# The attention pieces' plain fp32 products side by side, and one split product for the row of negative maxima

## The chip, the cores and the metric

The kernel runs on one core of a Trainium2 chip. The metric is the device time of one execution in microseconds; smaller is better. Of the kernel before there are three runs: 497.45, 497.55 and 498.71 us, median 497.55 us. Beside them stands one profiled execution, from which all rows below come.

## The reference, cut to what matters

One layer of a decoder trunk on 256 positions of width 1024. What touches the change is the mixer:

```python
proj = x @ w_in + b_in            # q_m k_m v_m o_m i_m f_m q_b k_b v_b g_a g_b
# mLSTM branch: 4 heads x 256, stabilised by a running maximum m_q
s   = (q @ k.T) * exp(d_intra - m_q)
num = s @ v ;  den = s.sum(-1)
h   = num / maximum(abs(den), exp(-m_q))
y_a = sigmoid(o_m) * head_norm(h)
# attention branch: 8 heads x 128, one block, causal, with a relative bias
p   = softmax(q @ k.T * scale + bias)
y_b = p @ v
merged = sigmoid(g_a) * (y_a @ w_branch_a) + sigmoid(g_b) * (y_b @ w_branch_b)
x = layer_norm(alpha * x + merged @ w_out)
x = layer_norm(alpha * x + conv_gated_mlp(x))
```

All of it is in fp32. With one layer and no state carried in, the maximum of a position is a running maximum over positions, one row of 256 numbers for each mLSTM head.

## The kernel before, in words

**Numbers.** A matmul in plain fp32 takes several passes on TensorE. For the large products the kernel therefore cuts each fp32 operand into a high part (rounded to the type float32r) and a low part (what is left), and adds three products of one pass: high x high, high x low and low x high. The helper `split_into` makes the parts: ScalarE (ACT in the profile) casts the high part, line 91, and VectorE (DVE) subtracts, line 92. The helper `mm3` issues the three products, lines 125 to 127. A few small products and all transposes stay plain fp32.

**Weights.** They come as 81 chunks of 1 MB in the order of `chunk_order`: four of the output gate `o`, then for each of four groups the eight chunks `qm, qb, km, kb, vm, vb, ga, gb`, then the branch products `wa, wb`, the output product `wo`, and the feed-forward chunks `up` and `dn`. SyncE (SP) issues their loads into three raw buffers, five chunks ahead (line 86). Each step of the loop in `run` first issues the element work (`elem_work`: what is left of the step before, and the splits of the chunk two steps ahead), then the load, then the chunk's 48 matmuls, and at the end the small TensorE pieces that `side_pe` holds for this step. The order of instructions on an engine is the order in which the program writes them.

**Start.** Before the loop, `run` loads x and the first chunks in pieces, splits chunks 0 and 1 (line 235) and issues the small loads. The identity matrix `ident` (line 225) is loaded by POOL's queue, behind two broadcasts of bias rows (lines 220 and 221), which wait for their own load. After them POOL clears some tiles, among them `nM` (line 274). The splits of chunk 2 come with the first `elem_work` of the loop.

**A group.** A group is two attention heads and one mLSTM head; its eight steps are b to b+7. The maxima are made once, in the first group, by `gates_schedule`: `e1d` (lines 566 to 570) writes the negated row of each head into partitions 0 to 3 of `nM`. In each group the small pieces are:

- at the end of step b+4: `pe_m` (line 603) lays the group's row on all 128 partitions by one plain product with a column of `ident`; `pe_s` makes the scores of the mLSTM head, of which the block of the later half is plain (line 612); `pe_l(0)` the logits of the first attention head, whose own block is plain (line 711)
- at the end of b+5: `pe_l(1)` for the second head, and `pe_n`, scores x v
- at the end of b+6: `pe_t`, six transposes of the probabilities (line 744)
- at the end of b+7: `pe_y`, four transposes of the mLSTM output (line 695), then `pe_o`, probabilities x v, where each head has one plain product between its split ones (lines 760 to 763)
- in the element work of b+8: `el_y`, then `el_o`, which evacuate these two for the branch products. In the last group b+8 is the first `wa` step, which reads the result of `el_y`.

The side products use five PSUM banks in turn (`ps_side`), the large ones three (`ps_main`).

**Memory.** Pools lie on top of each other from the left: `const` first, then `stream` (raw and split chunks), then the others. `yah, yal, ybh, ybl` and the split parts of the first two `up` chunks lie in pools on the right side. Tiles that TensorE reads carry pads, which the helper `after` and the function `shift` set.

Of the kernel before, what the change touches and what calls it, by code (L numbers as in the profile page):

```python
# [69 lines left out]
class Kernel:  # L70
# [103 lines left out]
    def run(self):  # L174
# [95 lines left out]
        self.cbuf = mp.tile([P, 2, S + 3], F32, name="cbuf")  # L270
        g.memset(self.cbuf[:, :, 0:3], 0.0)

        self.nM = mp.tile([P, S], F32, name="nM")
        g.memset(self.nM, 0.0)
        self.toe = mp.tile([P, 2, S], F32, name="toe")
        self.cv = {n: mp.tile([P, 2, S], F32, name="cv" + n) for n in ("qm", "km")}
        self.ones4 = xp.tile([4, 2 * S], F32, name="ones4")
# [249 lines left out]
    def gates_schedule(self, bif):  # L527
        nc, mp = self.nc, self.xp
        st = {}
        v = nc.vector  # L530

        def e0():
            gt = mp.tile([P, 2, 8], F32, name="gt")
            for t in range(2):
                v.tensor_add(gt[:, t, :], self.psg[t][:, 256:264], bif)
            st["gt"] = gt

        def p0():
            ps = self.ps_side([4, 2, S], "ps_gt")
            for w in range(2):  # L540
                for t in range(2):
                    nc.tensor.transpose(ps[:, w, t * P:(t + 1) * P], st["gt"][:, t, 4 * w:4 * w + 4], self.ident)
            st["ps"] = ps

        def e1():
            ps = st["ps"]
            big = mp.tile([P, KT, S], F32, tag="xraw", name="gates")
            fs, t1, F, G, M, nFM, nM = (big[0:4, k, :] for k in range(7))
            v.tensor_copy(fs, ps[:, 1, :])
            v.scalar_tensor_tensor(t1, fs, -1.0, fs, op0=ALU.mult, op1=ALU.min)  # L550
            nc.scalar.activation(t1, t1, AF.Exp)
            nc.scalar.activation(t1, t1, AF.Ln, bias=1.0)
            st["g"] = fs, t1, F, G, M, nFM, nM

        def e1b():
            fs, t1, F, G, M, nFM, nM = st["g"]
            one = self.ones4[:, 0:S]
            v.scalar_tensor_tensor(fs, fs, 0.0, t1, op0=ALU.min, op1=ALU.subtract)
            v.tensor_tensor_scan(F, one, fs, 0.0, op0=ALU.mult, op1=ALU.add)

        def e1c():
            fs, t1, F, G, M, nFM, nM = st["g"]
            v.tensor_sub(G, st["ps"][:, 0, :], F)
            v.tensor_tensor_scan(M, self.ones4[:, S:2 * S], G, 0.0, op0=ALU.max, op1=ALU.max)

        def e1d():
            fs, t1, F, G, M, nFM, nM = st["g"]
            v.tensor_scalar(self.nM[0:4, :], M, -1.0, None, op0=ALU.mult)
            v.scalar_tensor_tensor(nFM, F, -1.0, M, op0=ALU.mult, op1=ALU.subtract)
            st.update(G=G, nFM=nFM)  # L570

        def p1():
            ps = self.ps_side([P, 2, 2, 4], "ps_gc")
            for w, n in enumerate(("G", "nFM")):
                for t in range(2):
                    nc.tensor.transpose(ps[:, w, t, :], st[n][:, t * P:(t + 1) * P], self.ident[0:4, 0:4])
            st["gc"] = ps

        def e2():
            self.gcol = self.const.tile([P, 2, 4], F32, name="gcol")  # L580
            self.floor = self.const.tile([P, 2, 4], F32, name="floor")
            v.tensor_copy(self.gcol, st["gc"][:, 0])
            self.floor_exp = lambda: nc.scalar.activation(self.floor, st["gc"][:, 1], AF.Exp)

        b = self.start_g[0]
        self.side_elem.setdefault(b, []).append(e0)
        self.side_pe.setdefault(b, []).append(p0)
        self.mixed[b + 1] = lambda w: w + [None, None, e1]
        self.mixed[b + 2] = lambda w: w + [e1b, None, e1c, None, e1d]
        self.side_pe.setdefault(b + 3, []).append(p1)  # L590
        self.mixed[b + 4] = lambda w: w + [e2]


    def group_schedule(self, g):
# [5 lines left out]
        def pe_m():  # L600

            psw = self.ps_side([P, S], f"psw{g}")
            nc.tensor.matmul(psw, self.ident[:, g:g + 1].to_broadcast([P, P]), self.nM, start=True, stop=True)
            st["psw"] = psw

        def pe_s():
            qh, ql = self.hl["qm"]
            kh, kl = self.hl["km"]
            pss = self.ps_side([P, 2, S], f"pss{g}")

            for k in range(2):
                nc.tensor.matmul(pss[:, 0, P:], self.cv["km"][:, k, P:], self.cv["qm"][:, k, P:],
                                 start=k == 0, stop=k == 1)
            for k in range(2):
                self.mm3(pss[:, 1, :], kh[:, k, 0:P], kl[:, k, 0:P], qh[:, k, :], ql[:, k, :], k == 0, k == 1)
            st["pss"] = pss
# [81 lines left out]
        def el_y():  # L698
            for j in range(2):
# [3 lines left out]
                v.scalar_tensor_tensor(self.yal[:, c, :], st["psy"][:, j, :], gain, self.yah[:, c, :].bitcast(F32),  # L703
                                       op0=ALU.mult, op1=ALU.subtract)

        def pe_l(i):
            qh, ql, qf = self.qb
            kh, kl = self.hl["kb"]
            ps = self.ps_side([P, 2, S], f"psl{g}_{i}")

            nc.tensor.matmul(ps[:, 0, 0:P], qf[:, i, :], self.kbf[:, i, :], start=True, stop=True)
            self.mm3(ps[:, 1, :], qh[:, i, :], ql[:, i, :], kh[:, i, :], kl[:, i, :], True, True)
            st["l", i] = ps

        def el_l(i):
            h = 2 * g + i
# [34 lines left out]
            a.copy(tf, ps[:, 2, :])  # L751

        def pe_o():
            ps = self.ps_side([P, 2, S], f"pso{g}")
            vh, vl, vf = self.vb
            for i in range(2):
                th, tl, tf = self.pt[i]
                c = slice(i * P, (i + 1) * P)
                mm = nc.tensor.matmul
                mm(ps[:, i, :], vh[:, c], th, start=True, stop=False)  # L760
                mm(ps[:, i, P:], vf[:, c], tf, start=False, stop=False)
                mm(ps[:, i, :], vh[:, c], tl, start=False, stop=False)
                mm(ps[:, i, :], vl[:, c], th, start=False, stop=True)
            st["o"] = ps

        def el_o():
            ps = st["o"]
            for i in range(2):
                h = 2 * g + i
                bias = self.vec[:, V_BVB + h:V_BVB + h + 1]  # L770
                a.activation(self.ybh[:, h, :], ps[:, i, :], AF.Identity, bias=bias)
                v.scalar_tensor_tensor(self.ybl[:, h, :], ps[:, i, :], bias, self.ybh[:, h, :].bitcast(F32),
                                       op0=ALU.add, op1=ALU.subtract)

        def at(where, k, f):
# [6 lines left out]
        at(self.side_pe, 4, pe_m)  # L782
        at(self.side_pe, 4, pe_s)
        at(self.side_pe, 4, lambda: pe_l(0))
        at(self.side_pe, 5, lambda: pe_l(1))
        at(self.side_pe, 5, pe_n)
        self.mixed[b + 5] = lambda w: [w[0], el_w, lambda: el_l(0), w[1], lambda: el_e(0), el_s, lambda: el_l2(0),
                                       el_s2] + w[2:]
# [2 lines left out]
        at(self.side_pe, 6, lambda: pe_t(0))  # L791
        at(self.side_pe, 6, lambda: pe_t(1))
        self.mixed[b + 6] = lambda w: [lambda: el_l(1), lambda: el_e(1), el_n1] + w + [lambda: el_l2(1), el_n1b]
        at(self.side_pe, 7, pe_y)
        at(self.side_pe, 7, pe_o)
        self.mixed[b + 7] = lambda w: [lambda: el_t(0), el_n2, lambda: el_t(1)] + w
        at(self.side_elem, 8, el_y)
        at(self.side_elem, 8, el_o)


    def open_post(self, pp):
# [375 lines left out]
```

## Time and profile before

| what | value |
|---|---|
| runs | 497.45, 497.55, 498.71 us; median 497.55 |
| span of the profiled execution | 495.6 us, 9471 instructions |
| the profiled execution's own time | its span of 495.6 us, and by the median 1.9 us around it |
| PE (TensorE matmul) busy | 484.4 us, 98% of the span |
| DVE busy, ACT busy, POOL busy | 369.2, 288.5, 29.1 us |
| split product, one pass, 128x256 in `wa` | 64 records, mean 276 ns each, overlapping |
| plain product of the row, 128x256 | two records each, 8 in four groups, mean 378 ns |
| plain product or transpose, 128x128 | mean 272 to 274 ns for a record |

A record's length on PE holds its way through the array, which the next one overlaps. What one matmul costs is therefore read from start to start, or from the chain of waits, where each piece stands with what it adds. The page's 40 slices show PE at nine tenths or more from the second slice on to the last but one.

### The profile page before, as it was taken

To read this page: it belongs to the slowest core of one execution; us is meant where nothing else is said; L and a number is where in the kernel's file an instruction comes from. 1 tells how busy PE (TensorE), PEld (TensorE's weight loads), DVE (VectorE), ACT (ScalarE), POOL (GpSimd) and SP (SyncE) were. 2 spreads that over 40 slices of the span, in tenths; PEclk is the share of its full clock that TensorE was granted. 3 is DMA by queue.
4 is the path that set the end of the run, shared out by engine and by line. 5 is a ranking of instruction groups with operands and counts; after the bars stand their busy time and mean duration, and the time that the engine had idled before them with its cause. 6 is when DMAs were issued, how large, how long until landed. Compare 5 with 4: busy or idle time off the path is not lost.

```text
span 495.6 us, 9471 instructions
## 1 busy us (share of the span) xinstructions
PE 484.4 (98%) x3889; PEld 468.0 (94%) x3889; DVE 369.2 (74%) x662; ACT 288.5 (58%) x479; POOL 29.1 (6%) x46
## 2 busy tenths in 40 slices
PE   8999999999999999999999999999999999999992
PEld 4899999999999999999999999999999999999982
DVE  5676995888588858885677788888667766866886
ACT  6567867496658665866655524766554555554610
POOL 0400011001100110002000001000000000000001
PEclk9999999999999999999999999999999999999998
DMA  8984555556554645443945572646555456444202
GB/s 251 351 305 153 202 197 200 175 173 193 184 184 171 196 172 196 172 171 136 371 176 179 221 280 86 255 145 212 203 206 175 165 181 245 170 171 171 86 1 85
DMA packets 19036, 93.74 MB, mean 189 GB/s; under 512 B 4625, under 2 KB 5913, under 8 KB 9009
## 3 DMA queue, kind: packets, MB, share of 16 engines
q1 hardware_dynamic: 14834, 87.08, 49.2%
q0 software_dynamic: 4160, 6.07, 3.9%
q8 instruction: 30, 0.49, 0.4%
q14 instruction: 12, 0.10, 0.1%
HBM read 92.05 MB, written 2.63 MB: 191 GB/s over the span
## 4 chain that ended last, share of the span: by engine, by line
PE 94%; DMA 2%; DVE 1%; SPq 1%; ACT 0%; issue 0%; POOL 0%; POOLq 0%
PE ps_up L127 8%; PE ps_up L126 8%; PE ps_up L125 8%; PE ffn L127 4%; PE ffn L126 4%; PE ffn L125 4%; PE ps_vm L125 2%; PE ps_vm L127 2%; PE ps_qm L125 2%; PE ps_vm L126 2%; PE ps_ga L127 1%; PE ps_ga L125 1%; PE ps_vb L126 1%; PE ps_vb L127 1%; PE ps_vb L125 1%; PE ps_ga L126 1%
## 5 line engine op out<-in xcount | busy, mean ns | idle before, releaser
L92 DVE TENSOR_TENSOR wl<-raw,wh 128x1024 fp32r<-128x1024 f32 (+1 forms) x162 | 187.5, 1197 | 29.2 <-ACT wh L91 29.0
L91 ACT CAST wh<-raw 128x1024 fp32r<-128x1024 f32 (+1 forms) x162 | 158.8, 1030 | 11.6 <-DMA raw<-in_wst_dram 6.3
L127 PE MATMUL ps_up<-x1h,wl 128*128 128x256 f32 x320 | 89.9, 281 | 0.0
L126 PE MATMUL ps_up<-x1l,wh 128*128 128x256 f32 x320 | 89.9, 281 | 0.0
L125 PE MATMUL ps_up<-x1h,wh 128*128 128x256 f32 x319 | 89.7, 281 | 0.0
L126 PEld LDWEIGHTS ps_up<-x1l,wh 128*128 128x128 f32 x320 | 61.4, 192 | 0.0
L127 PEld LDWEIGHTS ps_up<-x1h,wl 128*128 128x128 f32 x320 | 60.1, 188 | 0.0
L125 PEld LDWEIGHTS ps_up<-x1h,wh 128*128 128x128 f32 x319 | 59.9, 188 | 0.0
L1010 DVE SCALAR_TENSOR_TENSOR cu<-ps_up,vec,cu 128x255 f32<-128x255 f32 (+1 forms) x80 | 33.0, 475 | 27.1 <-ACT cu L1006 26.9
L127 PE MATMUL ffn<-wh,hl 128*128 128x512 f32 (+1 forms) x110 | 38.4, 349 | 0.0
L126 PE MATMUL ffn<-wl,hh 128*128 128x512 f32 (+1 forms) x110 | 38.4, 349 | 0.0
L125 PE MATMUL ffn<-wh,hh 128*128 128x512 f32 (+1 forms) x110 | 38.3, 349 | 0.0
L91 ACT CAST hh<-cu 128x256 fp32r<-128x256 f32 x22 | 8.9, 407 | 42.8 <-DVE cu L1018 42.8
L1006 ACT ACTIVATE cu<-ps_up,vec 128x256 f32<-128x256 f32 x40 | 16.8, 472 | 28.8 <-PE ps_up L127 28.0
L126 PEld LDWEIGHTS ffn<-wl,hh 128*128 128x128 f32 x110 | 20.8, 189 | 3.0
L125 PEld LDWEIGHTS ffn<-wh,hh 128*128 128x128 f32 x110 | 20.7, 188 | 3.0
L127 PEld LDWEIGHTS ffn<-wh,hl 128*128 128x128 f32 x110 | 20.7, 188 | 2.9
L125 PE MATMUL ps_gb<-xth,wh 128*128 128x256 f32 x64 | 18.0, 282 | 0.0
L126 PE MATMUL ps_vm<-wl,xth 128*128 128x256 f32 x64 | 17.9, 280 | 0.0
L127 PE MATMUL ps_vm<-wh,xtl 128*128 128x256 f32 x64 | 17.9, 280 | 0.0
L125 PE MATMUL mix<-wh,mgh 128*128 128x256 f32 x64 | 17.8, 279 | 0.0
L125 PE MATMUL ps_qm<-xth,wh 128*128 128x256 f32 x64 | 17.8, 278 | 0.0
(295 smaller groups left out, 1428.9 us busy)
## 6 DMA issues: line engine op xcount, KB each, us to landing
raw<-in_wst_dram SPq DMA_DIRECT2D x78, 1024.0 KB, 4.9
raw<-in_wst_dram SPq DMA_DIRECT2D x8, 256.0 KB, 4.5
lnrow<-in_rows_dram POOLq DMA_DIRECT2D x4, 512.0 KB, 7.5
band<-table POOLq DMA_DIRECT2D x4, 384.0 KB, 13.0
xraw<-in_xt_dram SPq DMA_DIRECT2D x8, 128.0 KB, 4.3
raw<-in_wst_dram SPq DMA_DIRECT2D x2, 512.0 KB, 7.6
toe<-band POOLq DMA_DIRECT2D x4, 256.0 KB, 4.2
xtok<-in_x_dram POOLq DMA_DIRECT2D x1, 1024.0 KB, 8.3
```

The source lines that it names most:

```text
L91: self.nc.scalar.copy(wh, raw)
L92: self.nc.vector.tensor_sub(wl, raw, wh.bitcast(F32))
L125: mm(ps, ah if first is None else first, bh, start=start, stop=False)
L126: mm(ps, ah, bl, start=False, stop=False)
L127: mm(ps, al, bh, start=False, stop=stop)
L1006: act.activation(cu[:, j, :], ps[:, j, :], AF.Copy, scale=tap(2, j))
L1010: v.scalar_tensor_tensor(cu[:, j, o:], ps[:, j, :S - o], tap(t, j), cu[:, j, o:], op0=ALU.mult, op1=ALU.add)
```

## The change

- `nM` becomes float32r. `e1d` writes the negated row into a plain tile, ACT copies its high part into partitions 0 to 3 of `nM`, and DVE subtracts and writes the low part into partitions 32 to 35. A new tile `pick` of four columns, in the `const` pool, has a one in row g and in row 32 + g of column g; DVE makes it at the start by adding two slices of `ident`. `pe_m` then is one float32r product, which adds high and low part.
- The own blocks of both heads' logits go behind the plain part of the scores (`pe_l_own`, called in `pe_s`), and `pe_l(1)` moves from step b+5 to b+4.
- `pe_o` has one PSUM tile for each head and issues the split products of both heads, then the two plain ones; `pe_y` comes after it. `el_o` comes before `el_y`.

```diff
-        self.nM = mp.tile([P, S], F32, name="nM")
-        g.memset(self.nM, 0.0)
+        self.nM = mp.tile([P, S], F32R, name="nM")
+        g.memset(self.nM.bitcast(F32), 0.0)
+        self.pick = const.tile([P, 4], F32R, name="pick")
+        nc.vector.tensor_add(self.pick, ident[:, 0:4], ident[:, 32:36])
...
         def e1d():
             fs, t1, F, G, M, nFM, nM = st["g"]
-            v.tensor_scalar(self.nM[0:4, :], M, -1.0, None, op0=ALU.mult)
+            v.tensor_scalar(nM, M, -1.0, None, op0=ALU.mult)
+            nc.scalar.copy(self.nM[0:4, :], nM)
+            v.tensor_sub(self.nM[32:36, :], nM, self.nM[0:4, :].bitcast(F32))
             v.scalar_tensor_tensor(nFM, F, -1.0, M, op0=ALU.mult, op1=ALU.subtract)
...
-            nc.tensor.matmul(psw, self.ident[:, g:g + 1].to_broadcast([P, P]), self.nM, start=True, stop=True)
+            nc.tensor.matmul(psw, self.pick[:, g:g + 1].to_broadcast([P, P]), self.nM, start=True, stop=True)
...
+            for i in range(2):
+                pe_l_own(i)
             for k in range(2):
                 self.mm3(pss[:, 1, :], kh[:, k, 0:P], kl[:, k, 0:P], qh[:, k, :], ql[:, k, :], k == 0, k == 1)
...
+        def pe_l_own(i):
+            ps = st["l", i] = self.ps_side([P, 2, S], f"psl{g}_{i}")
+            nc.tensor.matmul(ps[:, 0, 0:P], self.qb[2][:, i, :], self.kbf[:, i, :], start=True, stop=True)
+
         def pe_l(i):
             qh, ql, qf = self.qb
             kh, kl = self.hl["kb"]
-            ps = self.ps_side([P, 2, S], f"psl{g}_{i}")
-
-            nc.tensor.matmul(ps[:, 0, 0:P], qf[:, i, :], self.kbf[:, i, :], start=True, stop=True)
-            self.mm3(ps[:, 1, :], qh[:, i, :], ql[:, i, :], kh[:, i, :], kl[:, i, :], True, True)
-            st["l", i] = ps
+            self.mm3(st["l", i][:, 1, :], qh[:, i, :], ql[:, i, :], kh[:, i, :], kl[:, i, :], True, True)
...
         def pe_o():
-            ps = self.ps_side([P, 2, S], f"pso{g}")
+            ps = [self.ps_side([P, S], f"pso{g}_{i}") for i in range(2)]
             vh, vl, vf = self.vb
+            mm = nc.tensor.matmul
             for i in range(2):
                 th, tl, tf = self.pt[i]
                 c = slice(i * P, (i + 1) * P)
-                mm = nc.tensor.matmul
-                mm(ps[:, i, :], vh[:, c], th, start=True, stop=False)
-                mm(ps[:, i, P:], vf[:, c], tf, start=False, stop=False)
-                mm(ps[:, i, :], vh[:, c], tl, start=False, stop=False)
-                mm(ps[:, i, :], vl[:, c], th, start=False, stop=True)
+                mm(ps[i], vh[:, c], th, start=True, stop=False)
+                mm(ps[i], vh[:, c], tl, start=False, stop=False)
+                mm(ps[i], vl[:, c], th, start=False, stop=False)
+            for i in range(2):
+                mm(ps[i][:, P:], vf[:, i * P:(i + 1) * P], self.pt[i][2], start=False, stop=True)
             st["o"] = ps
...
         at(self.side_pe, 4, lambda: pe_l(0))
-        at(self.side_pe, 5, lambda: pe_l(1))
+        at(self.side_pe, 4, lambda: pe_l(1))
...
+        at(self.side_pe, 7, pe_o)
         at(self.side_pe, 7, pe_y)
-        at(self.side_pe, 7, pe_o)
...
+        at(self.side_elem, 8, el_o)
         at(self.side_elem, 8, el_y)
-        at(self.side_elem, 8, el_o)
```

More of the change, by code (lines that the diff above doesn't have):

```diff
@@ L770, in el_o @@
                 bias = self.vec[:, V_BVB + h:V_BVB + h + 1]
-                a.activation(self.ybh[:, h, :], ps[:, i, :], AF.Identity, bias=bias)
-                v.scalar_tensor_tensor(self.ybl[:, h, :], ps[:, i, :], bias, self.ybh[:, h, :].bitcast(F32),
+                a.activation(self.ybh[:, h, :], ps[i], AF.Identity, bias=bias)
+                v.scalar_tensor_tensor(self.ybl[:, h, :], ps[i], bias, self.ybh[:, h, :].bitcast(F32),
                                        op0=ALU.add, op1=ALU.subtract)
```

## The prediction

> **What bounds the kernel now.** I read the page's busy times first, then the chain of waits that ended last, then PE's waits, then the timelines of DVE, POOL and PE over the first 25 us.
>
> ```profile
> PE 484.4 (98%) x3889; PEld 468.0 (94%) x3889; DVE 369.2 (74%) x662; ACT 288.5 (58%) x479; POOL 29.1 (6%) x46
> ...
> PE 94%; DMA 2%; DVE 1%; SPq 1%; ACT 0%; issue 0%; POOL 0%; POOLq 0%
> ...
> PE warm_ps L196 <- DVE warm L193: 1.2, 1, 1.2
> PE ps_o L159 <- ACT wh L91: 0.9, 2, 0.7
> ```
>
> PE is busy for 98% and carries 94% of the chain. It waits 2.1 us in all, and only before the second chunk of weights is through. So work taken off PE comes off the end one for one, and a stall put into PE goes onto the end one for one: nothing later has slack to take it back.
>
> The profiled execution spans 495.6 us against a median of 497.55, so 1.9 us lies around the span. I sum against 495.6 and add 1.9.
>
> **Part 1: one product less in plain fp32.** These are pieces of the chain in group 1 (start, length, what):
>
> ```profile
> 110.31 0.12 PE ps_vm L127
> 110.43 0.43 PE psw L603 x2
> ```
>
> The row of maxima costs 0.43 us now, as two passes over 256 columns. As one split product it is one pass of 256 columns like its neighbour, 0.115 us. Saved: 0.315 us x 4 groups = 1.26 us.
>
> **Part 2: fewer changes between plain fp32 and split work.** Runs of plain fp32 or transposes per group now: row+scores, own block 0, own block 1, probability transposes, y transposes, two in the output product: 7. After: scores + both own blocks, probability transposes, two tails + y transposes: 3. So 16 fewer in all. What is one worth? PE's timeline around one of them:
>
> ```profile
> 111.85 0.39 PE L711 MATMUL psl<-kbf,qbf 128*128 128x128 f32 x2
> 112.00 0.36 PE L125 MATMUL psl<-kbh,qbh 128*128 128x256 f32 x1
> 112.20 0.28 PE L126 MATMUL psl<-kbl,qbh 128*128 128x256 f32 x1
> ...
> 112.67 0.28 PE L127 MATMUL ps_vb<-wh,xtl 128*128 128x256 f32 x1
> 112.78 0.28 PE L125 MATMUL ps_vb<-wh,xth 128*128 128x256 f32 x1
> ```
>
> The two plain passes and the split one after them end at 112.20 after 0.35 us. Two passes of 0.11 (half of 0.215, for half the columns) and one of 0.115 make 0.335, so at least 0.01 is the change itself. Up to 112.67 it took 0.82 us, where 0.22 + 5 x 0.113 = 0.785: with the next four matmuls it is 0.035 at most. I take 0.025: 16 x 0.025 = 0.4 us (0.2 to 0.55). Moving the second head's logits one step earlier moves PE work and adds none.
>
> **Part 3: the addition that makes the pick columns.** It stands after the splits of chunks 0 and 1 and before those of chunk 2 on DVE, and it reads ident. DVE now, then POOL:
>
> ```profile
> 15.35 0.69 DVE L92 TENSOR_TENSOR wl<-raw,wh 128x512 fp32r<-128x512 f32 x1 [1.62 <-ACT wh L91]
> 17.61 2.95 DVE L92 TENSOR_TENSOR wl<-raw,wh 128x1024 fp32r<-128x1024 f32 x2 [1.57 <-ACT wh L91]
> 21.65 2.36 DVE L92 TENSOR_TENSOR wl<-raw,wh 128x1024 fp32r<-128x1024 f32 x2 [1.10 <-ACT wh L91]
> ```
>
> ```profile
> 15.87 1.34 POOL L220 PARTITION_BROADCAST bo<-sga  x1 [15.37 <-DMA sga<-in_rows_dram]
> 17.09 1.30 POOL L221 PARTITION_BROADCAST bvm<-sga  x1
> 18.22 0.86 POOL L225 DMA_DIRECT2D ident<-in_ident_dram  x1
> ...
> 20.91 0.12 POOL L268 MEMSET vmh<- 128x4 f32 x1
> ```
>
> and the load of ident, from the instructions of its tile:
>
> ```profile
> L225 POOL DMA_DIRECT2D ident<-in_ident_dram x1: 860/860/860, 18.2 to 18.2; - x1
> DMA to landing us min/median/max: 5.1/5.1/5.1
> ```
>
> Ident is issued at 18.2, behind two broadcasts, and lands at 18.2 + 5.1 = 23.3. The engines keep the written order: POOL's memset of line 268 needs nothing, yet sat behind the broadcasts until 20.91. So DVE stands from 16.0 to 23.3, where it now makes chunk 2's low halves from 17.61. The addition itself (128x4) is like this row, 0.09 us:
>
> ```profile
> 35.14 0.09 DVE L535 TENSOR_TENSOR gt<-ps_o,bif 128x8 f32<-128x8 f32 x1
> ```
>
> Queued behind it are the low halves of chunks 2 and 3. One 1024-wide half takes 2.36/2 = 1.2 us. Who waits for that is PE:
>
> ```profile
> 19.04 0.28 PE L125 MATMUL ps_o<-wh,xth 128*128 128x256 f32 x1
> 19.38 0.39 PE L126 MATMUL ps_o<-wl,xth 128*128 128x256 f32 x1
> ```
>
> The second matmul of chunk 2 takes wl and starts as soon as its first half is there. It will start at 23.3 + 0.1 (wait seen) + 0.1 (addition) + 1.2 + 0.05 = 24.75 instead of 19.38: **5.4 us** of stall. The second half follows 1.2 us later, when PE has twelve matmuls of 0.118 in hand. Chunk 3's low halves come at 25.9 + 2.4 + 0.2 = 28.5; PE needs the first of them after 48 matmuls of chunk 2, about 30.5. The load of chunk 5 waits for chunk 2's buffer and slips by the same 5.3 us; chunk 5 is used three steps after chunk 2. So the stall is paid once and whole. Bounds: 4.5 if ident lands 0.9 earlier (its own 0.86 us of issue), 6.0 with a first half as slow as the 1.7 us which the first of the two in 2.95 can have taken.
>
> **Part 4: the clock after that stall.** PE is idle from 19.15 to 24.75. The trace has an idle stretch at the end, after the last matmul (columns: us, busy of PE, PEld, DVE, ACT, POOL, clock, DMA):
>
> ```profile
> 486.60:491.00 4.40, 0.00 (x0) 0.00 (x0) 3.56 (x10) 0.60 (x1) 1.86 (x3) 1.00 0.00 0
> 491.10:495.60 4.50, 0.00 (x0) 0.00 (x0) 1.19 (x2) 0.00 (x0) 0.42 (x1) 0.50 0.32 117
> ```
>
> After 4.4 us of idle the clock fell to half; 5.6 us is longer. At half clock a pass of 512 columns took 0.43, at full clock 0.23:
>
> ```profile
> 8.79 0.63 PE L159 MATMUL ps_o0b<-wh,xtl 128*128 128x512 f32 x1
> 9.22 0.63 PE L159 MATMUL ps_o<-wl,xth 128*128 128x512 f32 x1
> 9.64 0.45 PE L159 MATMUL ps_o0b<-wl,xth 128*128 128x512 f32 x1
> 9.93 0.39 PE L159 MATMUL ps_o<-wh,xth 128*128 128x512 f32 x1
> 10.16 0.40 PE L159 MATMUL ps_o0b<-wh,xth 128*128 128x512 f32 x1
> ```
>
> So about 45% of the time at half clock is lost. The clock rose near 9.8 there; PE had worked since 1.25 with breaks until 7.3, so a rise takes between 2.4 and 8.5 us of work. I take 4.5: 0.45 x 4.5 = **2.0 us** (1.1 to 3.8; nothing if it doesn't fall). The Trainium skill, "TensorE: Matmul & The Clock Gate", Part 1, says that the gate looks at free-running windows of 3.4 us and halves the clock after a whole idle one. The 4.4 us above agree. By that rule a 5.6 us gap holds a whole window in (5.6 - 3.4)/3.4 = 0.65 of the cases, an estimate from that page.
>
> **Part 5: small waits.** In the gates' chain the row is now copied on ACT between two DVE instructions. ACT has that copy between these two rows, and DVE makes its input only at 52.28:
>
> ```profile
> 47.15 1.98 ACT L91 CAST wh<-raw 128x1024 fp32r<-128x1024 f32 x2
> 49.04 0.82 ACT L418 ACTIVATE cbuf<-ps_km,vec 128x256 f32<-128x256 f32 x2
> ...
> 52.28 0.28 DVE L568 TENSOR_SCALAR nM<-gates 4x256 f32<-4x256 f32 x1
> ```
>
> So ACT's evacuation of km, 2 us of splits, and the table load and Silu behind them slip by 3.5 us; ACT has gaps that give back about half. The plain copy of kb then ends near the moment at which group 0 wants it: 0 to 1.0 us, once; I take 0.2. In group 3 y now comes after o on PE, ACT and DVE. These are ACT's y and the o behind it:
>
> ```profile
> 232.86 0.48 ACT L702 ACTIVATE yah<-psy,vec 128x256 fp32r<-128x256 f32 x1 [0.55 <-DVE yal L703]
> 234.28 0.48 ACT L771 ACTIVATE ybh<-pso,vec 128x256 fp32r<-128x256 f32 x1 [0.58 <-DVE ybl L772]
> 234.88 0.28 PE L125 MATMUL ps_wa<-yah,wh 128*128 128x256 f32 x1
> ```
>
> Going last, yah of the last chunk ends about 234.7 and its low half 235.2. The branch product wants them at 234.88 and 234.99: 0 to 0.4, I take 0.2. The second head's logits no longer stand between v and the product with the scores, which starts 0.35 us earlier. It has the room: the low part of the scores ends 2.7 us ahead of it.
>
> ```profile
> 115.20 0.55 DVE L640 TENSOR_TENSOR spl<-wt,sph 128x384 fp32r<-128x384 f32 x1
> 118.46 0.28 PE L125 MATMUL psn<-vmh,sph 128*128 128x258 f32 x1
> ```
>
> **Part 6: the pitch of the streams.** Two rows of one shape:
>
> ```profile
> L125 PE MATMUL ps_up<-x1h,wh 128*128 128x256 f32 x319 | 89.7, 281 | 0.0
> L125 PE MATMUL ps_wa<-yah,wh 128*128 128x256 f32 x64 | 17.7, 276 | 0.0
> ```
>
> Whole steps run at one pitch or the other, about 5 ns apart, and what decides it the trace doesn't say. The change adds a tile to the lowest pool, which shifts the pools above it but not those on the right side (yah, ybh, the first two up chunks), and it changes what goes before some steps. Loss at most: 384 branch matmuls + 96 up matmuls x 5 ns = 2.4 us. Gain at most: the 959 of up (three such groups) x 5 ns = 4.8 us. Nearest row is the same stream before, so I take 0.
>
> **Sum.** 495.6 + 1.9 + 5.4 + 2.0 + 0.4 - 1.26 - 0.4 = **503.6 us**, slower by 1.2%.
>
> **The rivals.**
> - *The stall without the fall of the clock.* All of the above but part 4: 503.6 - 2.0 = 501.6. For it: the idle stretch is only 1.2 us longer than the one after which the clock fell, and one fall is all that the trace shows.
> - *The addition's wait is hidden, and the change does what it says.* 497.5 - 1.26 - 0.4 + 0.4 = 496.2, faster. It decides from the point at which ident lands before 17.5 us, when DVE's next split has its input anyway. Against it: issue alone comes at 18.22, behind broadcasts that wait for their own load until 15.87.
> - *The pitch turns.* With the stall, and all of up at the faster pitch: 503.6 - 4.8 = 498.8, no loss after all. If the branch products and first up chunks take the slower one: 503.6 + 2.4 = 506.0. For both: equal shapes run at both pitches here. Against: up has one mean over all its 319.
>
> **How the numbers follow.** Stall with the fall of the clock 0.52, 503.6. Stall without 0.27, 501.6. Hidden wait 0.09, 496.2. Pitch for the better 0.04, 498.8; for the worse 0.08, 506.0. What a measurement can't tell from no change is 0.3%, 496.1 to 499.0. Faster 0.07 (most of the hidden case, which lies at that edge), same 0.06 (the rest of it and the better pitch), slower 0.87. The range runs from 500.2, the stall at its short bound without the clock, to 506.3, which takes in the worse pitch and most of a long rise of the clock.
>
> **What would show it.** In the profile after, DVE has an idle stretch of some 7 us that ends at 23 to 24 us with ident as releaser, in front of the addition; PE has one of about 5.5 us before the wl matmul of chunk 2; the clock over the next stretch is well under 1.00. The row's product takes one record of 256 columns, and there are 3 runs of plain fp32 in a group. I am wrong if DVE's addition starts before 18 us, if PE's stall is under 4 us, or if a later PE wait shrinks by what the stall added.

## The result and the profile after

Five runs after: 499.62, 500.01, 501.13, 503.11 and 504.19 us, median 501.13. Five runs before: 496.36 to 498.99 us, median 497.55. The ratio is 1.0076, with an interval of 1.0049 to 1.0103: slower by 3.6 us, where 6.1 was forecast. The profiled execution after spans 498.1 us, 2.5 more than the one before.

The page after, busy times and the chain by engine:

```profile
PE 481.7 (97%) x3885; PEld 465.9 (94%) x3885; DVE 368.8 (74%) x664; ACT 287.5 (58%) x480; POOL 29.2 (6%) x46
...
PE 93%; DMA 3%; DVE 1%; SPq 1%; POOL 1%; issue 0%; POOLq 0%
```

PE works 2.7 us less and the execution is still longer: a wait stands in the chain. PE's waits after, all of them (columns: us in all, times, longest):

```profile
PE ps_o L126 <- DVE wl L92: 4.5, 1, 4.5
PE ps_o L159 <- ACT wh L91: 1.6, 2, 0.9
PE warm_ps L196 <- DVE warm L193: 1.2, 1, 1.2
```

The first is new; the other two stand in the profile before too, with 0.9 us for the casts of ACT where there are 1.6 now. No wait is listed in group 0 or at the first `wa` step. DVE's timeline after shows who makes PE wait (columns: start, length, what, then in brackets the idle time before it and what ended that):

```profile
14.60 0.69 DVE L92 TENSOR_TENSOR wl<-raw,wh 128x512 fp32r<-128x512 f32 x1 [0.48 <-ACT wh L91]
22.92 0.16 DVE L276 TENSOR_TENSOR pick<-ident 128x4 fp32r<-128x4 f32 x1 [7.62 <-DMA ident<-in_ident_dram]
23.00 4.63 DVE L92 TENSOR_TENSOR wl<-raw,wh 128x1024 fp32r<-128x1024 f32 x4
```

DVE stands for 7.62 us in front of an addition of four columns, and what ends that is the load of `ident`. POOL's timeline after, then the load's time from issue to landing, from the tile's own view:

```profile
16.78 1.30 POOL L220 PARTITION_BROADCAST bo<-sga  x1 [16.28 <-DMA sga<-in_rows_dram]
17.96 1.30 POOL L221 PARTITION_BROADCAST bvm<-sga  x1
19.09 0.86 POOL L225 DMA_DIRECT2D ident<-in_ident_dram  x1
```

```profile
DMA to landing us min/median/max: 3.8/3.8/3.8
```

Issued at 19.09, landed at 22.9. And PE's timeline across the stall:

```profile
19.45 0.28 PE L125 MATMUL ps_o<-wh,xth 128*128 128x256 f32 x1
24.28 0.39 PE L126 MATMUL ps_o<-wl,xth 128*128 128x256 f32 x1 [4.55 <-DVE wl L92]
24.50 0.28 PE L127 MATMUL ps_o<-wh,xtl 128*128 128x256 f32 x1
...
25.00 0.41 PE L125 MATMUL ps_o<-wh,xth 128*128 128x256 f32 x1
25.21 0.41 PE L126 MATMUL ps_o<-wl,xth 128*128 128x256 f32 x1
```

Behind the stall the start-to-start time first is 0.12, then 0.21 us from 25.00 on: the clock has fallen. The windows after around that (columns: us, then busy of PE, PEld, DVE, ACT, POOL, then the granted clock, DMA share, GB/s):

```profile
21.53:24.94 3.41, 0.66 (x5) 0.66 (x6) 2.02 (x3) 2.99 (x5) 1.18 (x9) 1.00 0.15 48
24.94:28.35 3.41, 3.41 (x18) 3.41 (x17) 3.41 (x6) 1.12 (x1) 0.00 (x0) 0.50 0.49 168
28.35:31.76 3.41, 3.41 (x31) 3.41 (x30) 3.32 (x6) 1.13 (x2) 0.00 (x0) 1.00 1.01 396
```

The clock is at half for exactly the stretch 24.94 to 28.35: 18 matmuls where the next stretch has 31.

The change itself did what it says. The row and its neighbours in group 1 after:

```profile
116.13 0.28 PE L607 MATMUL psw<-nM,pick 128*128 128x256 f32 x1
116.25 0.60 PE L616 MATMUL pss<-cvqm,cvkm 128*128 128x128 f32 x4
116.69 0.61 PE L714 MATMUL psl<-kbf,qbf 128*128 128x128 f32 x4
117.06 0.36 PE L125 MATMUL pss<-qmh,kmh 128*128 128x256 f32 x1
```

One record of 256 columns, 0.12 us to the next start, and the plain products side by side.

**Where the time went.** The program has the same stages before and after, so their starts can be laid side by side. PE's timeline before, the matmuls with which the groups, the branch products, the output product and the feed-forward part begin, and the last matmul:

```profile
31.66 0.39 PE L125 MATMUL ps_qm<-xth,wh 128*128 128x256 f32 x1
...
232.50 0.28 PE L125 MATMUL ps_wa<-yah,wh 128*128 128x256 f32 x1
...
276.03 0.28 PE L125 MATMUL mix<-wh,mgh 128*128 128x256 f32 x1
...
298.71 0.28 PE L125 MATMUL ps_up<-aheadh,x1h 128*128 128x256 f32 x1
...
486.30 0.28 PE L127 MATMUL ffn<-wh,hl 128*128 128x256 f32 x1
```

The same five after:

```profile
38.11 0.39 PE L125 MATMUL ps_qm<-xth,wh 128*128 128x256 f32 x1
...
237.10 0.36 PE L125 MATMUL ps_wa<-yah,wh 128*128 128x256 f32 x1
...
282.75 0.28 PE L125 MATMUL mix<-wh,mgh 128*128 128x256 f32 x1
...
305.44 0.28 PE L125 MATMUL ps_up<-aheadh,x1h 128*128 128x256 f32 x1
...
488.78 0.28 PE L127 MATMUL ffn<-wh,hl 128*128 128x256 f32 x1
```

| stage | before, us | after, us | difference |
|---|---|---|---|
| until the groups begin | 31.66 | 38.11 | +6.45 |
| four groups | 200.84 | 198.99 | -1.85 |
| branch products `wa, wb` | 43.53 | 45.65 | +2.12 |
| output product | 22.68 | 22.69 | 0 |
| feed-forward, to the last matmul | 187.59 | 183.34 | -4.25 |
| last matmul starts | 486.30 | 488.78 | +2.48 |

The start splits further. PE came to chunk 2 at 19.45 instead of 19.04 (0.41, ahead of the wait); it stood 24.28 - 19.45 = 4.83 instead of 19.38 - 19.04 = 0.34 (4.49); and from the second matmul of chunk 2 to the groups it took 13.83 instead of 12.28 (1.55, the half clock).

The surprise is in the two other large rows. Neither the branch products nor the feed-forward matmuls are touched by the change, and PE doesn't wait in them. The same groups after as the prediction quotes of before:

```profile
L125 PE MATMUL ps_up<-x1h,wh 128*128 128x256 f32 x319 | 88.1, 276 | 0.0
L125 PE MATMUL ps_wa<-yah,wh 128*128 128x256 f32 x64 | 18.1, 282 | 0.0
```

Before it was 281 for `up` and 276 for `wa`. By the pitch, which is the time from one matmul's start to the next, the two streams have changed places: `up` is 4.4 ns a matmul faster (4.25 us / 960, the `up` matmuls without those of the first two chunks), the branch products 5.5 ns slower (2.12 us / 384).

### The profile page after: what moved, and what is told of

Its sections match the earlier page's. It is cut to its first block, busy times and chain, and to the rows that moved or that the text cites. A ratio compares the mean times of both kernels' runs of the same rounds, so it can differ in the third digit from the quotient of the medians.

```text
span 498.1 us, 9463 instructions
## 1 busy us (share of the span) xinstructions
PE 481.7 (97%) x3885; PEld 465.9 (94%) x3885; DVE 368.8 (74%) x664; ACT 287.5 (58%) x480; POOL 29.2 (6%) x46
## 4 chain that ended last, share of the span: by engine, by line
PE 93%; DMA 3%; DVE 1%; SPq 1%; POOL 1%; issue 0%; POOLq 0%
PE ps_up L126 8%; PE ps_up L127 8%; PE ps_up L125 8%; PE ffn L126 4%; PE ffn L127 4%; PE ffn L125 4%; PE ps_vm L125 2%; PE ps_wb L125 2%; PE ps_wa L125 2%; PE ps_wb L126 2%; PE ps_wa L127 2%; PE ps_wa L126 2%; PE ps_wb L127 2%; PE ps_vm L127 2%; PE ps_vm L126 2%; PE ps_qm L125 2%
## 5 line engine op out<-in xcount | busy, mean ns | idle before, releaser
L126 PE MATMUL ps_up<-x1l,wh 128*128 128x256 f32 x320 | 88.3, 276 | 0.0
L127 PE MATMUL ps_up<-x1h,wl 128*128 128x256 f32 x320 | 88.3, 276 | 0.0
L125 PE MATMUL ps_up<-x1h,wh 128*128 128x256 f32 x319 | 88.1, 276 | 0.0
L126 PEld LDWEIGHTS ps_up<-x1l,wh 128*128 128x128 f32 x320 | 60.1, 188 | 0.0
L1017 DVE SCALAR_TENSOR_TENSOR cu<-ps_up,vec,cu 128x255 f32<-128x255 f32 (+1 forms) x80 | 33.1, 476 | 23.4 <-ACT cu L1013 23.4
L125 PE MATMUL ps_wa<-yah,wh 128*128 128x256 f32 x64 | 18.1, 282 | 0.0
```

The lines of the kernel that those rows point to most:

```text
L125: mm(ps, ah if first is None else first, bh, start=start, stop=False)
L126: mm(ps, ah, bl, start=False, stop=False)
L127: mm(ps, al, bh, start=False, stop=stop)
L1017: v.scalar_tensor_tensor(cu[:, j, o:], ps[:, j, :S - o], tap(t, j), cu[:, j, o:], op0=ALU.mult, op1=ALU.add)
```

## The experiments

The theory after this: the load of `ident` costs the start some 6 us (stall and clock), the rearranged pieces give 1.85, and the new tile, which moves the pools above it by 32 bytes, makes `up` faster and `wa, wb` slower. The rival for the first: something else in the change holds DVE. The rival for the last: the order of the pieces does it, or it differs from one execution to the next.

**pick_late.** The addition goes from the start into the first piece of the gates' chain. Nothing else moves.

```diff
         self.pick = const.tile([P, 4], F32R, name="pick")
-        nc.vector.tensor_add(self.pick, ident[:, 0:4], ident[:, 32:36])
...
         def e0():
+            v.tensor_add(self.pick, self.ident[:, 0:4], self.ident[:, 32:36])
```

> The changed kernel, but the addition that makes the pick columns is issued with the first addition of the gates' chain (near 35 us on DVE), long after ident has landed; its tile keeps its place. Theory (the wait of DVE for ident costs 4.5 us of PE stall and the fall of the clock 1.7 us): 501.1 - 6.2 = 494.9 us, no PE idle before chunk 2's low product, clock 1.00 from 10 us on. Rival (the loss comes from the pitch of the streams or from the reordered pieces, and the stall is taken back later): 500 to 501 us.

Measured: 494.39 us, ratio to the kernel before 0.9939 (0.9924 to 0.9954). The addition now takes its place without a wait, as the view of its line shows:

```profile
L534 DVE TENSOR_TENSOR pick<-ident x1: 85/85/85, 36.9 to 36.9; 128x4 fp32r<-128x4 f32 x1
```

The groups begin at 33.40; every later stage has the length it has in the kernel after, to 0.01 us. So the wait for `ident`, with the fall of the clock behind it, is the whole loss, and the change without it is faster than the kernel before.

**layout_32.** The kernel before, with a tile of the size of `pick` at the same place, which nobody reads:

```diff
+        self.spare = const.tile([P, 4], F32, name="spare")
+        g.memset(self.spare, 0.0)
```

> The kernel before, with a 32-byte tile added to the lowest pool and nothing else (POOL clears it). Theory (the place of the pools sets the pitch of the streams): the branch products go from 276 to 281 ns a record, 384 x 5 ns = 1.9 us lost, the first two up chunks lose up to 0.4, the other up chunks go from 281 to 276, 959 x 4.5 ns = 4.3 us gained: 497.55 - 2.0 = 495.5 us. Rival (what is issued before a step sets its pitch): both rows stay as before, 497.5 us.

Measured: 495.59 us, ratio 0.9957 (0.994 to 0.9974). 32 unused bytes make the kernel before 2 us faster. Two groups of it:

```profile
L126 PE MATMUL ps_up<-x1l,wh 128*128 128x256 f32 x320 | 88.3, 276 | 0.0
...
L126 PE MATMUL ps_wa<-yal,wh 128*128 128x256 f32 x64 | 17.9, 280 | 0.0
```

The feed-forward part takes 183.34 us as in the kernel after, the branch products 45.05 instead of 43.53, and the output product, which the change left alone, 23.42 instead of 22.68. So the exchange of pitches needs none of the change's instructions.

**ident_wait.** The kernel before, with the early addition into a spare tile of another pool, which leaves the tiles that TensorE streams where they were (`xp` is the program's name of that pool):

```diff
+        early = xp.tile([P, 4], F32, name="early")
+        nc.vector.tensor_add(early, ident[:, 0:4], ident[:, 32:36])
```

> The kernel before, with one addition of two slices of ident into a spare tile at the place where the change makes its pick columns, and no tile that matmuls of the streams read is moved. Theory: DVE stands until ident lands near 22.8 to 23.3, PE stalls 4.5 to 5.4 us, the clock falls in most executions and costs up to 2 more: 502 to 504.5 us. Rival (the wait is hidden or taken back): 497.5 us.

Measured: 505.6 us, ratio 1.0164 (1.0145 to 1.0184), so 8 us for one addition of four columns. All stages from the groups on are those of the kernel before to 0.01 us; only the start is longer, 38.95 instead of 31.66. That is 1.1 us above the expected 502 to 504.5. In the trace PE goes on with chunk 2 at 24.34 instead of 19.38, 4.96 later, where 4.5 to 5.4 was expected. PE's timeline, then the windows, columns as above:

```profile
17.96 0.28 PE L125 MATMUL ps_o<-wh,xth 128*128 128x256 f32 x1
24.34 0.58 PE L126 MATMUL ps_o<-wl,xth 128*128 128x256 f32 x1 [6.10 <-DVE wl L92]
```

```profile
19.34:22.75 3.41, 0.00 (x0) 0.00 (x0) 0.00 (x0) 2.14 (x3) 3.35 (x12) 1.00 0.82 333
22.75:26.16 3.41, 1.82 (x8) 1.82 (x9) 3.18 (x4) 3.28 (x3) 0.00 (x0) 0.50 0.01 2
26.16:29.57 3.41, 3.41 (x18) 3.41 (x17) 3.41 (x6) 0.51 (x1) 0.00 (x0) 0.50 0.84 305
29.57:32.98 3.41, 3.41 (x31) 3.41 (x30) 2.49 (x4) 0.96 (x2) 0.00 (x0) 1.00 0.98 344
```

Here the clock is at half for two stretches, and PE works through 5.2 us of them (24.34 to 29.57) against 3.4 in the kernel after. From the second matmul of chunk 2 to the groups it took 38.95 - 24.34 = 14.61 us instead of 12.28, so 2.33 for the clock, where up to 2 was expected. The other 0.8 of the runs' 8.1 us is not explained.

**layout_128.** pick_late with a `pick` of 128 bytes instead of 32 to a partition, which moves the pools above by 128 (the four columns are 16 bytes and take up 32):

```diff
-        self.pick = const.tile([P, 4], F32R, name="pick")
+        self.pick = const.tile([P, 32], F32R, name="pick")[:, 0:4]
```

> The changed kernel with the late addition, and with the pick tile widened to 128 bytes, so that the pools move by 128 bytes and not by 32. Theory (the place modulo 128 bytes sets the pitch): branch products back at 276 ns, up back at 281; left are the two gains, 1.26 for the row's product and 0.4 for fewer changes between plain and split work: 495.9 us. Rival (the new order of the pieces set the pitch): up stays at 276 and the branch products at 281, as in the late kernel, near 494.9 us.

Measured: 499.42 us, ratio 1.0037 (1.0024 to 1.005), a miss by 3.5 us. The feed-forward part went back to its slow 187.39 us, as the theory of place says; but the branch products stayed slow at 45.31, and the output product became slow, 23.42. All three are on the slower side at once, in a kernel that has the rearranged pieces and tiles that lie as they did before, modulo 128 bytes.

**row_split_alone.** layout_32 with the split product for the row (and the late addition), but the order of the attention pieces as before.

```diff
+        self.pick = const.tile([P, 4], F32R, name="pick")
...
-            nc.tensor.matmul(psw, self.ident[:, g:g + 1].to_broadcast([P, P]), self.nM, start=True, stop=True)
+            nc.tensor.matmul(psw, self.pick[:, g:g + 1].to_broadcast([P, P]), self.nM, start=True, stop=True)
```

> The kernel moved by 32 bytes (layout_32) with the split row product alone, its pick columns made late; the own blocks, the output product and the y transposes stand as before. Theory: of the 1.65 us by which the four groups got shorter between layout_32 and the late kernel (200.64 to 198.99 us), 1.26 belong to the row's product: 199.4 us from the first qm matmul to the first branch product. Rival (the order of the pieces brings most of it): 200.2 us or more.

Measured, one run: 494.15 us. The groups take 199.36 us where layout_32 takes 200.64: 1.28 for the four products. The kernel after has 198.99, so the order of the pieces is worth 0.37.

**ident_early.** The kernel after with its early addition, but the load of `ident` goes first in POOL's queue, ahead of the broadcasts:

```diff
+        nc.gpsimd.dma_start(ident, self.ident_d)
...
-        for t, d in ((ident, self.ident_d), (vec, self.vec_d), (rel, self.rel_d), (onehot, self.onehot_d)):
+        for t, d in ((vec, self.vec_d), (rel, self.rel_d), (onehot, self.onehot_d)):
```

> The changed kernel with the addition where it is, but the load of ident is issued first on POOL's queue, ahead of the broadcasts. Theory (DVE waits for that load and nothing else): ident lands before 10 us, DVE and PE don't stand, as with the late addition: 494.4 us. Rival (the addition at that place hurts in another way, or the early load takes time from the loads of x): over 496 us.

Measured: 494.72 us, ratio 0.9936 (0.9915 to 0.9956). The tile's view (columns of the lines: shortest, median and longest in ns, then first and last start):

```profile
L210 POOL DMA_DIRECT2D ident<-in_ident_dram x1: 740/740/740, 1.3 to 1.3; - x1
L277 DVE TENSOR_TENSOR pick<-ident x1: 1126/1126/1126, 17.0 to 17.0; 128x4 fp32r<-128x4 f32 x1
...
DMA to landing us min/median/max: 4.0/4.0/4.0
```

The load takes about as long as in the kernel after, 4.0 us against 3.8, but from 1.3 on. The addition itself takes 1.13 us at that place, and no wait of PE on DVE is listed. Place of the load and place of the addition cure the same loss, to ratios of 0.9936 and 0.9939, so nothing clear of the noise is left of it for another cause.

**late_aligned.** pick_late with the pads of the branch chunks and of the first `up` chunks changed, so that they lie modulo 128 bytes as in the kernel before, relative to what they are multiplied with.

```diff
-        return 56
+        return 16
...
-                        zp.tile([P, 2112], F32R, name=f"ahead{n}{j}")[:, 8:8 + 2048] for n in "hl")
+                        zp.tile([P, 2112], F32R, name=f"ahead{n}{j}")[:, 16:16 + 2048] for n in "hl")
```

> The kernel with the late addition, and the pads of what lies next to the right side set anew: 16 elements for the branch weights instead of 56 (32 - 160 = -128 bytes against yah, so modulo 128 as in the kernel before) and 16 instead of 8 for the first two up chunks (they move by 32 bytes like the pools on the left). Theory (the place modulo 128 of the two operands against each other sets the pitch): branch products back from 45.6 to 43.5 us, up stays fast: 494.4 - 2.1 = 492.3 us. Rival (what is issued just before the branch products sets their pitch, as the slow ones of the kernel moved by 128 bytes say): they stay at 45.3 or more, 494 us.

Measured: 498.42 us, ratio 1.0015 (1.0001 to 1.0028): no gain, a miss by 6 us. The branch products stayed slow at 45.31, as the rival said, and `up`, whose own tiles lie as in pick_late, became slow:

```profile
L126 PE MATMUL ps_up<-x1l,wh 128*128 128x256 f32 x320 | 89.9, 281 | 0.0
```

So the place of a stream's own two operands modulo 128 bytes does not decide its pitch, and the theory of place fell in that form.

**late_aligned_y_first.** The same, with `pe_y` again ahead of `pe_o` and `el_y` ahead of `el_o`.

```diff
+        at(self.side_pe, 7, pe_y)
         at(self.side_pe, 7, pe_o)
-        at(self.side_pe, 7, pe_y)
...
+        at(self.side_elem, 8, el_y)
         at(self.side_elem, 8, el_o)
-        at(self.side_elem, 8, el_y)
```

> As late_aligned, but the y transposes stand before the output products again, and the y evacuation before that of the output. Theory of the place: branch products at 43.5 us in both; this one 0.02 x 4 us slower for one more change between plain and split work in each group, 492.4 us. Rival (what is issued just before sets the pitch): branch products at 43.5 here and at 45.3 in late_aligned, so this one is about 1.8 us faster than that.

Measured: 493.99 us, ratio 0.9919 (0.9895 to 0.9943), the lowest time of all. But not for the reason expected: the branch products are still at 45.31. The output product is fast (22.69), and the feed-forward part takes 183.62, because most of `up` went at the faster pitch:

```profile
L126 PE MATMUL ps_up<-x1l,wh 128*128 128x256 f32 x320 | 88.5, 276 | 0.0
```

The groups are 0.37 longer than in late_aligned, where 0.08 was expected; 0.21 of it is the chunk `vb` of the first group, 5.66 us here and 5.45 there, so that a stream in the groups turned as well. What was changed stands some 68 us ahead of the first `up`. That suggested that a stream takes over its pitch from what goes before.

**merged, merged_aligned, merged_128.** In `pe_o` the transposes of `pe_y` stand next to the plain products, with split products ahead and behind, so that the branch products follow split work. merged has the tiles as in pick_late, merged_aligned the pads of late_aligned, merged_128 the wider `pick`.

```diff
                 mm(ps[i], vh[:, c], th, start=True, stop=False)
+            for i in range(2):
+                mm(ps[i][:, P:], vf[:, i * P:(i + 1) * P], self.pt[i][2], start=False, stop=False)
+            pe_y()
+            for i in range(2):
+                th, tl, tf = self.pt[i]
+                c = slice(i * P, (i + 1) * P)
                 mm(ps[i], vh[:, c], tl, start=False, stop=False)
-                mm(ps[i], vl[:, c], th, start=False, stop=False)
-            for i in range(2):
-                mm(ps[i][:, P:], vf[:, i * P:(i + 1) * P], self.pt[i][2], start=False, stop=True)
+                mm(ps[i], vl[:, c], th, start=False, stop=True)
...
-        at(self.side_pe, 7, pe_y)
...
+        at(self.side_elem, 8, el_y)
         at(self.side_elem, 8, el_o)
-        at(self.side_elem, 8, el_y)
```

> As late_aligned, but the output product issues its first split products, then the two plain ones, then the y transposes, then its other four split products, and y is evacuated first; so four split matmuls and no plain ones stand before the branch products. Theory (a stream takes its pitch over from what runs before it, and the fast one holds where the two operands lie as in the kernel before): branch products 43.5 us instead of 45.3, the output product 22.7 instead of 23.4; up, if it follows, 168.2 instead of 172.5: 492.0 us, or 496 if only the first two follow. Rival (the pitch has nothing to do with what runs before): 498.4 us as late_aligned.

> The same order of the output product and the y transposes in the late kernel with its pads unchanged (branch weights 32 bytes off against yah). Theory: where the operands lie 32 bytes off, no order gives the fast pitch, the branch products stay at 45.0 to 45.7 us and the rest as in the late kernel: 494.4 us. Rival (the order alone sets it): branch products at 43.5, 492.3 us.

> The same order in the kernel whose pools are moved by 128 bytes (layout_128). Theory: the branch products go from 45.3 to 43.5 us, the output product from 23.4 to 22.7, and up stays slow at 172.5 as in the kernel before: 496.9 us. Rival (the pitch has nothing to do with what runs before): 499.4 us as layout_128.

Measured: merged_aligned 497.87 us, ratio 0.9999 (0.9988 to 1.001); merged 494.51, ratio 0.9932 (0.991 to 0.9953); merged_128, one run, 497.21. The branch products took 45.23, 45.06 and 45.23 us: slow in all three, where 43.5 was expected of merged_aligned and merged_128, so split work just ahead of them doesn't make them fast. The feed-forward part took 187.58, 187.81 and 187.60.

That of merged doesn't fit its own median. Its profiled execution took 498.56 us; its other nine took 492.58 to 495.39. Was that one slow in `up`, and the nine not?

**merged_again.** The same program once more, for its trace.

> The same kernel as merged, for a second profile: there the profiled execution took 498.56 us with up at 172.5 us, the nine others 492.6 to 495.4. Theory (the pitch of a stream is not fixed by the program; it is taken up in each execution): this execution lies near 494.5 us, with up at 168.2 us and all the rest as in the first profile. Rival (the pitch is fixed by the program, and the first profile was slow for another reason): up at 172.5 us again, whatever the time.

Measured, one run: 494.42 us, beside 495.31 for one run of the kernel before, which has no trace and is the shortest of all that kernel's runs (the others: 496.36 to 499.32). The rows of `up`, first of merged, then of merged_again:

```profile
L126 PE MATMUL ps_up<-x1l,wh 128*128 128x256 f32 x320 | 89.9, 281 | 0.0
```

```profile
L126 PE MATMUL ps_up<-x1l,wh 128*128 128x256 f32 x320 | 88.4, 276 | 0.0
```

One program, two executions, two pitches: 187.81 and 183.50 us for the feed-forward part, while groups (199.09 both), branch products (45.06 and 45.07) and output product (23.42 and 23.41) agree. So the program alone does not fix the pitch of `up` in that kernel. The two profiles come from two chips. Against the chip as the cause stand merged's other nine runs, taken on the chip of its first profile: they lie 3.2 to 6.0 us below that execution, about what the faster `up` is worth (4.3), but have no trace.

The place where the two part can be read. The first `up` chunks are interrupted by eight transposes. These are the first `up` matmul behind them and the next `ffn` matmul, first in merged, then in merged_again:

```profile
315.52 0.36 PE L125 MATMUL ps_up<-x1h,wh 128*128 128x256 f32 x1
...
324.09 0.39 PE L125 MATMUL ffn<-wh,hh 128*128 128x512 f32 x1
```

```profile
315.79 0.37 PE L125 MATMUL ps_up<-x1h,wh 128*128 128x256 f32 x1
...
324.04 0.39 PE L125 MATMUL ffn<-wh,hh 128*128 128x512 f32 x1
```

From the first `up` of all to the one shown both took 16.1 us; the 72 matmuls from there on took 8.57 and 8.25. Just ahead of the transposes both went at the slow pitch, 0.12 us from start to start; merged_again came out of them at the faster one and kept it to the end. What chose it these rows don't say.

The lengths of the stages in all profiled executions, in us, each worked out from the starts of the five matmuls as above:

| kernel | groups begin | groups | branch | output | feed-forward | last matmul |
|---|---|---|---|---|---|---|
| before | 31.66 | 200.84 | 43.53 | 22.68 | 187.59 | 486.30 |
| after | 38.11 | 198.99 | 45.65 | 22.69 | 183.34 | 488.78 |
| pick_late | 33.40 | 198.99 | 45.65 | 22.69 | 183.35 | 484.08 |
| ident_early | 32.20 | 198.99 | 45.65 | 22.69 | 183.35 | 482.88 |
| ident_wait | 38.95 | 200.84 | 43.53 | 22.68 | 187.59 | 493.59 |
| layout_32 | 31.95 | 200.64 | 45.05 | 23.42 | 183.34 | 484.40 |
| row_split_alone | 31.41 | 199.36 | 45.05 | 23.42 | 183.50 | 482.74 |
| layout_128 | 32.50 | 199.01 | 45.31 | 23.42 | 187.39 | 487.63 |
| late_aligned | 31.89 | 198.99 | 45.31 | 23.42 | 187.59 | 487.20 |
| late_aligned_y_first | 31.79 | 199.36 | 45.31 | 22.69 | 183.62 | 482.77 |
| merged_aligned | 32.17 | 199.09 | 45.23 | 22.69 | 187.58 | 486.76 |
| merged | 31.82 | 199.09 | 45.06 | 23.42 | 187.81 | 487.20 |
| merged_again | 32.10 | 199.09 | 45.07 | 23.41 | 183.50 | 483.17 |
| merged_128 | 30.40 | 199.11 | 45.23 | 23.45 | 187.60 | 485.79 |

The first column differs by up to 3 us among kernels without the wait, so a difference in the start of two single executions means little below that. The variants were traced on four chips. The other columns fall on a few levels: the feed-forward part is near 183.4 or near 187.6, the output product 22.7 or 23.4.

## Why the prediction was right, and where it was wrong

The direction and the main cause held: slower, by a wait of DVE on `ident` that PE inherits, with a fall of the clock behind it. The median of 501.13 us lies in the range, 2.5 us below the forecast. That it does is in part luck: two streams turned that the forecast had at 0, and one turn gave back half of the other. With the gain of `up` alone the median would lie near 501.13 - 2.12 = 499.0, below the range. In the profiled executions the forecast was +6.1 and the trace has +2.5. Part by part:

- **Part 1, the row's product.** 1.26 us forecast; 1.28 by row_split_alone against layout_32.
- **Part 2, fewer changes between plain and split work.** 0.4 forecast; 0.37 by the kernel after against row_split_alone. The rest of the groups' 1.85 us, 0.20, is layout_32 against the kernel before: the pitch again.
- **Part 3, the wait for `ident`.** 5.4 forecast; 4.49 in the profiled execution. PE resumed at 24.28, not at 24.75, mostly since `ident` landed at 22.9 and not at 23.3: the load took 3.8 us instead of the 5.1 it took before, though POOL came to it 0.87 later. That is 0.47. The other 0.41 is that PE itself came late to chunk 2 in this execution. The value stands at the short end of the bounds, 4.5.
- **Part 4, the clock.** 2.0 forecast; 1.55 measured. The rise was taken as 4.5 us of work at half clock; it came after 3.4. In ident_wait it came after 5.2 and cost 2.33. The share lost at half clock is 0.45 in both (1.55 / 3.41 and 2.33 / 5.23), as forecast; what varies is the time at half clock. In ident_wait wait and clock together are 38.95 - 31.66 = 7.29 us (4.96 and 2.33), against 7.4 by the forecast. By the runs the two are worth 1.64% in ident_wait and 1.0076 - 0.9939 = 1.37% between after and pick_late, 6.8 to 8.2 us. So by the runs the sum of Parts 3 and 4 was about right; the traced execution of the kernel after has 6.04 of it. The five times after lie 4.6 us apart, those before 2.6; that this is the clock's phase is likely but not shown, as only one of the five has a trace.
- **Part 5, small waits.** 0.4 forecast; none is listed among PE's waits, and pick_late's groups give no sign of one.
- **Part 6, the pitch of the streams: the step that failed.** Taken at 0, "nearest row is the same stream before". What came was both ends of its bounds together: the branch products lost 2.12 us (of the 2.4 allowed, together with the first `up` chunks), and `up` gained 4.25 (of 4.8). The net is -2.1 us. With -1.4 for Parts 3 and 4, -0.4 for Part 5, -0.2 in the groups and +0.4 for PE's late arrival at chunk 2 that makes the 3.7 us by which the forecast was too high in the profiled executions. The prediction kept a rival for each sign and none in which the two streams move in opposite directions.

The rival without the fall of the clock came nearest in time, 501.6, and is wrong in its mechanism: the clock fell. The rival of the hidden wait gave 496.2 and is about what pick_late is, except that there the net gain of the streams, 2.1 us, came on top. The rival of the better pitch named half of what the streams did, at 0.04: it had the faster `up` and not the slower branch products.

What decides the pitch stays open. Place modulo 128 bytes alone fell with late_aligned and layout_128; the kind of work just ahead fell with the merged kernels; and merged with merged_again shows that in one kernel it differs between executions. What the runs do show: a matmul stream of this shape keeps one pitch through whole steps, `up` one of two; no wait of PE is listed at either; and edits of 32 bytes, or of the order of a few small products far ahead, went together with a turn of it that the runs carry (layout_32, late_aligned_y_first).

Five of the variants with several runs are faster than both kernels: late_aligned_y_first (493.99 us), pick_late (494.39), merged (494.51), ident_early (494.72) and layout_32 (495.59). The intervals of the first four overlap, so no order among them is shown.

## What to carry to other kernels

Before an instruction is put among the first ones of a busy engine, look up when its operands land and on whose queue they were issued: one addition of four columns cost the kernel before 8 us because its load stood behind two broadcasts, and moving either the load or the addition took that away. When an edit allocates a tile, compare the stages that it doesn't touch as well, since here 32 unread bytes were worth 2 us by themselves, more than the edit's own 1.65 (1.28 and 0.37). A single profile of such a kernel can show another pitch of a stream than most of its runs seem to have, so a stage's gain is believed when the runs carry it.

## What the runs showed of the hardware

**More than one pitch for one stream.** Split matmuls of 128x256 with no wait ran at about 113 or 118 ns from start to start in `up` (183.34 or 187.59 us for the same feed-forward work), and at 113 to 119 in the branch products (43.53 to 45.65 us for 384). One program did both in `up`, merged and merged_again.

**The clock fell without an empty window.** In the kernel after, the clock was halved at 24.94 although PE had worked 0.66 us in the 3.41 us before. Earlier in the same execution it fell after a stretch in which PE had been busy for more than half:

```profile
4.46:7.87 3.41, 1.83 (x7) 0.82 (x6) 1.67 (x4) 2.10 (x5) 0.00 (x0) 1.00 0.99 318
7.87:11.29 3.42, 3.42 (x10) 2.66 (x9) 2.73 (x7) 2.60 (x6) 0.00 (x0) 0.50 0.95 333
11.29:14.70 3.41, 3.41 (x17) 2.78 (x16) 2.91 (x7) 2.50 (x6) 0.00 (x0) 1.00 0.99 275
```

From PE's first matmul at 1.25 up to 7.87 its longest gap was 0.86 us, so no 3.41 us in between were idle. The share of work doesn't settle it either: 18.11 to 21.53 had 1.62 us of work and no fall behind it. In ident_wait 1.82 us of work in 3.41 did not bring the clock back; a full stretch did. The half-clock pieces lie on one grid: from 7.87 to 24.94 are five times 3.41 us. The Trainium skill, "TensorE: Matmul & The Clock Gate", Part 1, tells of free-running windows of 3413 ns, with the clock down after an idle one and up after a busy one. Length, grid and rise agree with these rows; an idle window ahead of each fall does not.
